# A retention and linear-attention layer on one core: the input projection by Strassen's scheme in groups of 512 columns, norm vectors on the activations, both gates at the end

## The chip, the cores and the metric

The kernel runs on one core of a Trainium2 chip. The metric is the device time of one execution in microseconds (us). The core has a matrix engine (TensorE, "PE" in the profile; its loads of the stationary operand are listed apart as "PEld"), a vector engine (VectorE, DVE), an activation engine (ScalarE, ACT), a general engine (GpSimd, POOL) and a queue that issues DMAs (SyncE, SP). Each engine takes its instructions strictly in the order in which they stand in its queue and waits on semaphores for the others. Matrix products are accumulated in PSUM (eight banks of 128 partitions x 512 float32); all else lies in SBUF.

## The reference: what is computed

One layer over 16 meta tokens and 512 tokens (T = 512, D = 1024). Cut to what matters:

```python
u = rms_norm(h, norm_gain)                 # (528, 1024)
proj = u @ w_in                            # w_in: 1024 x 11280
rq, rk, rv, rg, gq, gk, gv, gg, glr, m_ret, m_gla = split(proj)
# retention, 4 heads: q, k of 256 with rope, v and gate of 512, decay per head
o_ret = head_group_norm(retention(rope(rq), rope(rk), rv), ret_norm_gain) * silu(rg)
# gated linear attention (GLA), 4 heads: q, k of 128, v and gate of 256
log_a = log_sigmoid(glr @ w_gate_up + b_gate) / 16
o_gla = head_rms_norm(gla(gq, gk, gv, log_a), gla_norm_gain) * silu(gg)
merged = sigmoid(m_ret) * (o_ret @ w_branch_ret) + sigmoid(m_gla) * (o_gla @ w_branch_gla)
out = rms_norm(h + merged @ w_out, final_norm_gain)    # the 512 tokens
```

## The kernel before

Every large product is made of three passes in float32r: each operand is split exactly into a high and a low part (`split`, L132 to L134: a cast on ScalarE writes the high part, a subtraction on VectorE the low part), and `mm3` (L136 to L139) issues high x high, low x high and high x low into one PSUM bank. A product with 1024 rows of depth therefore takes 8 x 3 matmuls for each output tile of 128 rows.

The normalised activations stand transposed in SBUF, `uh` and `ul`: depth on partitions, 512 tokens and then 16 meta tokens in the free dimension. The weights are streamed from DRAM in tiles of 512 KB (`raw`, four buffers), each split into `_h` and `_l` tiles of 128x1024 (three buffers each). There are two forms of the projection:

- `proj_a` (L179) makes 256 columns with the columns on the partitions; the 512 tokens are the moving operand (N = 512), or 2 x 264 when the meta tokens are wanted (rk, gk). It serves rq, rk, gq, gk and the gates mr and mg.
- `proj_b` (L209) makes 512 columns with the tokens on the partitions; 512 weight columns are the moving operand (N = 512), 96 matmuls for the group. It serves rv, rg, gv, gg and the output projection wo. For rv and gv 16 small native-float32 matmuls (rv_pm, gv_pm) add the meta rows.

`branch` (L243) multiplies the gated output of an attention by its branch weights (br for a retention head, bg for a GLA pair): 96 matmuls with N = 512. Here the norm gains act on the weights: each quarter of a weight tile, 128x256, is scaled by ScalarE (L249) and by VectorE (L250) while it is split.

The order in time is written out by the generators: `weave` (L148) puts one step of a chain of small dependent work after each step of dense products. Then a scheduler orders each engine's queue from that. Stage by stage: gv0; gq0 and gk0 with the forget gates' chain (L344 to L392) woven into both; gg0 with GLA attention 0; gq1 and gk1 with the GLA output 0; gv1; gg1 and the branch bg0 with GLA attention 1; the gate mg (four `proj_a` of 256 columns) with GLA output 1; bg1, whose result is multiplied by the gate in `acc` (L584, L585); then for each head rq and rk (rope at L614; for heads 1 to 3 woven with the attention of the head before, followed by that head's branch br), rg with the scores, and rv; the gate mr with the attention of head 3; br3; wo.

The attention of a head (`ret_attention`, L698) makes four blocks of outputs (`av`, PE), their mean and variance (L715, L716), a small chain VectorE - GpSimd - VectorE, the normalised output on ScalarE (L721), the product with the gate (L722), and transposes (`ot`, L729) with a split.

PSUM is divided in two pools of four banks: `pp` for dense products, `pa` for the rest.

## Time and profile before

| | |
|---|---|
| time, median of 3 runs | 834.37 us (834.16 to 834.43) |
| span of the profiled execution | 832.0 us; its median time is 2.37 us above that |
| instructions in the trace | 10218 |
| longest stage by kind | a group of 512 columns takes 22 to 25 us of PE, and there are 21 such groups in the projection beside gv0 |
| DMA | 74.42 MB, 89 GB/s on average |

The page gives, for each engine, the time in which it was busy, its share of the span and its number of instructions. Matmuls are pipelined: the trace gives each a duration that is longer than the distance to the next one, so the pace of TensorE is read from the starts of consecutive matmuls and not from their durations. A group's row reads: line, engine, operation, output <- inputs (buffer numbers left out), shapes, count | busy us, mean ns of one | idle time of the engine just before them and what ended it. The stage table gives for a stretch of the span the busy time of each engine in it; "PEclk" is the clock granted to TensorE as a share of full speed.

### The profile page before, as it was taken

The page shows a single profiled execution, that of the slowest core. Times are in us where ns is not written, and L with a number is a line of the kernel's source. Part 1 is how long each engine was busy: PE and PEld are TensorE (multiplying, and loading weights), DVE is VectorE, ACT ScalarE, POOL GpSimd, SP SyncE. Part 2 cuts the span into 40 slices and gives each one's busy share as a digit, 9 for nine tenths or more (in the row PEclk, how much of TensorE's full clock was granted, in tenths as well). Part 3 has the DMA queues.
Part 4 walks back from the last instruction along what each step waited for, and adds up shares of the span by engine and source line. Part 5 has one row for each costly group of instructions (what it writes and reads, how often), then busy time and mean ns, then how long its engine had stood idle before and what let it go on. Part 6 is the DMA issues. An engine that isn't in the chain of part 4 may idle for free.

```text
span 832.0 us, 10218 instructions
## 1 busy us (share of the span) xinstructions
PE 814.9 (98%) x4018; PEld 665.2 (80%) x4018; DVE 420.4 (51%) x701; ACT 309.9 (37%) x563; POOL 119.6 (14%) x162
## 2 busy tenths in 40 slices
PE   7999999999999999999999999999999999999996
PEld 4779879778788889877988779888788887888885
DVE  3475564237542366415764247742467433546832
ACT  5473453245533323223432233322334233343422
POOL 5401330014300002100210002200022000221031
PEclk9999999999999999999999999999999999999999
DMA  8242110140223234214232051320512204242302
GB/s 259 67 145 78 51 52 26 60 144 27 74 79 99 81 105 146 74 39 145 60 97 68 26 176 51 102 76 26 177 51 87 92 26 145 84 176 76 126 1 101
DMA packets 57784, 74.42 MB, mean 89 GB/s; under 512 B 6708, under 2 KB 39732, under 8 KB 57736
## 3 DMA queue, kind: packets, MB, share of 16 engines
q1 hardware_dynamic: 57736, 73.78, 27.8%
q8 instruction: 31, 0.51, 0.3%
q14 instruction: 17, 0.14, 0.0%
HBM read 71.67 MB, written 2.10 MB: 89 GB/s over the span
## 4 chain that ended last, share of the span: by engine, by line
PE 92%; DVE 2%; ACT 2%; POOL 1%; issue 1%; DMA 1%; SPq 0%; POOLq 0%; DVEq 0%; ACTq 0%
PE rv_p L137 4%; PE rv_p L138 4%; PE rg_p L138 4%; PE rg_p L139 4%; PE rv_p L139 4%; PE rg_p L137 4%; PE br_p L138 4%; PE br_p L139 4%; PE br_p L137 3%; PE rk_p L137 2%; PE rk_p L138 2%; PE rk_p L139 2%; PE rq_p L137 2%; PE mr_p L137 2%; PE wo_p L138 2%; PE mg_p L139 2%
## 5 line engine op out<-in xcount | busy, mean ns | idle before, releaser
L145 POOL TENSOR_TENSOR g_r<-g_v,mhalf 128x1 f32<-128x1 f32 x16 | 8.8, 550 | 320.8 <-DVE g_v L144 320.8
L137 PE MATMUL rv_p<-rv_h,uh 128*128 128x512 f32 x128 | 50.9, 398 | 0.0
L138 PE MATMUL rv_p<-rv_l,uh 128*128 128x512 f32 x128 | 50.6, 396 | 0.0
L138 PE MATMUL rg_p<-rg_l,uh 128*128 128x512 f32 x128 | 50.6, 396 | 0.0
L139 PE MATMUL rg_p<-rg_h,ul 128*128 128x512 f32 x128 | 50.4, 394 | 0.0
L139 PE MATMUL rv_p<-rv_h,ul 128*128 128x512 f32 x128 | 50.4, 394 | 0.0
L137 PE MATMUL rg_p<-rg_h,uh 128*128 128x512 f32 x128 | 50.4, 394 | 0.0
L139 PE MATMUL br_p<-oh,br_l 128*128 128x512 f32 x128 | 50.2, 393 | 0.0
L138 PE MATMUL br_p<-ol,br_h 128*128 128x512 f32 x128 | 50.2, 392 | 0.0
L137 PE MATMUL br_p<-oh,br_h 128*128 128x512 f32 x128 | 49.8, 389 | 0.0
L134 DVE TENSOR_TENSOR rv_l<-rv_w,rv_h 128x1024 fp32r<-128x1024 f32 x16 | 19.6, 1226 | 42.7 <-ACT rv_h L133 42.2
L137 PE MATMUL rk_p<-uh,rk_h 128*128 128x264 f32 x128 | 37.1, 290 | 0.0
L138 PE MATMUL rk_p<-ul,rk_h 128*128 128x264 f32 x128 | 36.4, 284 | 0.0
L139 PE MATMUL rk_p<-uh,rk_l 128*128 128x264 f32 x128 | 36.3, 284 | 0.0
L250 DVE SCALAR_TENSOR_TENSOR br_l<-br_w,rgain,br_h 128x256 fp32r<-128x256 f32 x64 | 32.7, 555 | 5.8 <-ACT br_h L249 5.8
L133 ACT CAST rg_h<-rg_w 128x1024 fp32r<-128x1024 f32 x16 | 16.8, 1051 | 49.4 <-PE br_p L138 37.9
L249 ACT ACTIVATE br_h<-br_w,rgain 128x256 fp32r<-128x256 f32 x64 | 28.5, 501 | 11.8 <-PE mr_p L138 7.3
L721 ACT ACTIVATE on<-av,nm,g_r 128x512 f32<-128x512 f32 x16 | 12.5, 780 | 53.9 <-DVE nm L719 53.9
L137 PEld LDWEIGHTS rv_p<-rv_h,uh 128*128 128x128 f32 x128 | 24.0, 188 | 9.0 <-issue 3.4
L139 PEld LDWEIGHTS rv_p<-rv_h,ul 128*128 128x128 f32 x128 | 24.0, 187 | 5.8
L139 PEld LDWEIGHTS rg_p<-rg_h,ul 128*128 128x128 f32 x128 | 24.0, 188 | 5.6
L138 PEld LDWEIGHTS rv_p<-rv_l,uh 128*128 128x128 f32 x128 | 24.0, 188 | 5.4
(296 smaller groups left out, 2255.1 us busy)
## 6 DMA issues: line engine op xcount, KB each, us to landing
rg_w<-in_w_in_dram SPq DMA_DIRECT2D x16, 512.0 KB, 3.5
rv_w<-in_w_in_dram SPq DMA_DIRECT2D x16, 512.0 KB, 3.5
br_w<-in_w_branch_ret_dram SPq DMA_DIRECT2D x16, 512.0 KB, 3.9
gv_w<-in_w_in_dram SPq DMA_DIRECT2D x8, 512.0 KB, 7.2
gg_w<-in_w_in_dram SPq DMA_DIRECT2D x8, 512.0 KB, 3.6
bg_w<-in_w_branch_gla_dram SPq DMA_DIRECT2D x8, 512.0 KB, 3.5
mg_w<-in_w_in_dram SPq DMA_DIRECT2D x8, 512.0 KB, 3.7
rq_w<-in_w_in_dram SPq DMA_DIRECT2D x8, 512.0 KB, 4.3
```

Source lines behind the costliest of these rows:

```text
L133: nc.scalar.copy(hi, src)
L134: eng.tensor_sub(lo, src, hi.bitcast(F32))
L137: nc.tensor.matmul(o, lh, rh, start=first, stop=False)
L138: nc.tensor.matmul(o, lh, rl, start=False, stop=False)
L139: nc.tensor.matmul(o, ll, rh, start=False, stop=last)
L145: nc.gpsimd.tensor_tensor(r[:rows], v[:rows], mhalf[:rows], op=ALU.pow)
L249: nc.scalar.activation(hi[:, k, :], raw[:, k, :], AF.Copy, scale=g)
L250: nc.vector.scalar_tensor_tensor(lo[:, k, :], raw[:, k, :], g, hi[:, k, :].bitcast(F32), op0=ALU.mult, op1=ALU.subtract)
L721: nc.scalar.activation(on, ps, AF.Identity, scale=r, bias=nm)
```

## The change

**Quads.** The 21 groups of 512 columns other than gv0 (rq+rk, rg and rv of four heads; gq+gk of two pairs; gg0, gg1, gv1; mr and mg, two each) are made by a new function `quad`. The 1024-deep product of 512 tokens and 512 columns is cut in 2 x 2 blocks of 512 deep by 256, and seven products of blocks (numbered 1 to 7 in the code, issued in the order 1, 2, 7, 6, 5, 3, 4) stand for the eight. Each has 24 matmuls with N = 256, or 264 where the meta tokens are wanted ("wide"): 168 for the group. It first loads four blocks `blk[kh, n]` of 128x1024 into the ring of raw tiles. Its core:

```diff
+    def quad(cols, rows, name, evac, meta=None, wide=False):
...
+        product(1, A11, blk[0, 0], "b", True)
+        x1 = copy("b", 1)
+        run_late()
+        yield
+        t2 = wraw(f"{name}_t2")
+        product(2, A12, blk[1, 0], "a", True)
+        nc.vector.tensor_sub(blk[0, 0], blk[0, 1], blk[0, 0])
+        nc.vector.tensor_sub(blk[0, 1], blk[1, 1], blk[0, 1])
+        nc.vector.tensor_sub(t2, blk[1, 1], blk[0, 0])
+        out(0, 0, "a", x1)
+        yield
+        product(7, S3, blk[0, 1], "c", True)
+        yield
+        product(6, S2, t2, "b", False)
+        nc.vector.tensor_sub(blk[1, 0], blk[1, 0], t2)
+        x2 = copy("b", 2)
...
+        yield
+        product(5, S1, blk[0, 0], "b", False)
+        out(1, 1, "c", copy("b", 3))
+        run_late()
+        yield
+        product(3, S4, blk[1, 1], "b", False)
+        out(1, 0, "b", None)
+        yield
+        product(4, A22, blk[1, 0], "c", False)
+        out(0, 1, "c", x2)
+        yield
```

`product` splits its 128x1024 weights and accumulates 24 matmuls in a bank; products 1, 6, 5 and 3 accumulate in the same bank b, products 7 and 4 in bank c. `copy` is a ScalarE copy of bank b into SBUF between two of these products. `out` gives a quadrant of the result to the caller, with a bank and, for three of the four, a copy to be added to it on VectorE. The raw ring has six buffers instead of four; the `_h` and `_l` rings keep three.

**Activations.** In place of `uh` and `ul` there are the blocks A11, A12, A22 and A21 and the sums S1 to S4 of blocks, each split (`fh`, `fl`). The sums are formed once, behind the pre-norm: four VectorE operations and four splits.

**Norm vectors.** A function `turn` transposes the gated output of an attention by halves of the tokens and applies the gain while it splits (ScalarE 128x256 and VectorE 128x256, eight of each for a head), and `branch` now splits its weights plainly:

```diff
-            for k in range(4):
-                g = gain[:, gcol + k:gcol + k + 1]
-                nc.scalar.activation(hi[:, k, :], raw[:, k, :], AF.Copy, scale=g)
-                nc.vector.scalar_tensor_tensor(lo[:, k, :], raw[:, k, :], g, hi[:, k, :].bitcast(F32),
-                                               op0=ALU.mult, op1=ALU.subtract)
+            split(hi, lo, raw)
```

**Gates.** mg moves from the GLA part to the end, behind mr: `gates()` makes mr0, mr1, mg0, mg1 as quads, woven with the attention of head 3. The GLA branch's sum is stored to DRAM (`kept`) and loaded again at the end; GLA output 1 now runs between the attention and bg1 with nothing woven in:

```diff
-    weave(gate_gla(range(KD // 2)), gla_output(1))
-    drain(gla_branch(1))
+    drain(gla_output(1))
+    drain(gla_branch(1))
...
-    weave(gate_ret(), ret_attention(3))
+    weave(gates(), ret_attention(3))
```

**How the order of the work moves.** Queue rows: PE 3767 to 5008, DVE 624 to 878, ACT 471 to 672, POOL 133 to 146, SP 160 to 170. Three places:

VectorE in the first group with q and k of the GLA (gq0, gk0), where the forget gates' chain is woven in (la, fg_z and acc are its tiles; gq_6_l is the low part of product 6's weights). Before, only the last block of the chain stood among the gk splits:

```order
L134 TENSOR_TENSOR gvm_l<-gv_pm,gvm_h 128x512
L382 TENSOR_SCALAR la<-z_540 128x512
L385 TENSOR_SCALAR fg_z<-sigm 128x512
L134 TENSOR_TENSOR gk_0_l<-gk_0_w,gk_0_h 128x1024
L386 SCALAR_TENSOR_TENSOR fg_z<-fg_z,sigm 128x512
L134 TENSOR_TENSOR gk_1_l<-gk_1_w,gk_1_h 128x1024
L387 TENSOR_TENSOR la<-la,fg_z 128x512
L392 TENSOR_TENSOR la<-la,sigm 128x512 x5
```

In the changed kernel the rows from the last blocks of the chain to its end are:

```order
L491 TENSOR_SCALAR la<-z_622 128x512
L496 TENSOR_TENSOR la<-la,fg_z 128x512
L494 TENSOR_SCALAR fg_z<-acc 128x512
L513 TENSOR_TENSOR gq_570<-gq_a_641,gq_x_610 128x256
L495 SCALAR_TENSOR_TENSOR fg_z<-fg_z,acc 128x512
L513 TENSOR_TENSOR gq_570<-gq_a_642,gq_x_610 128x256
L496 TENSOR_TENSOR la<-la,fg_z 128x512
L141 TENSOR_TENSOR gq_6_l<-gq_t_636,gq_6_h 128x1024
L141 TENSOR_TENSOR gq_5_l<-gq_w_572,gq_5_h 128x1024
L501 TENSOR_TENSOR la<-la,acc 128x512 x5
L141 TENSOR_TENSOR gq_3_l<-gq_w_578,gq_3_h 128x1024
```

The whole chain (its first rows stand just ahead of these) now lies between the start of this group and product 6's low part, and its last five rows ahead of product 3's.

ScalarE in the gates, at the change from one group to the next. Before, a cast of weights and the sigmoid of a bank alternate with the attention's work (sigr is the gate, oh the transposed output):

```order
L133 CAST oh_5798<-ot_5986 128x4x128
L758 ACTIVATE sigr_5926<-mr_p_5933 128x512
L133 CAST oh_5798<-ot_6014 128x4x128
L133 CAST mr_0_h<-mr_0_w 128x1024
L758 ACTIVATE sigr_5926<-mr_p_5973 128x512
L133 CAST mr_1_h<-mr_1_w 128x1024
```

Now, from product 4's weights of mr1 to product 7's of mg0 (mr1_x2 and mr1_x3 are the copies of bank b behind products 6 and 5):

```order
L140 CAST mr1_4_h_7574<-mr1_w10_7378 128x1024
L228 COPY mr1_x2_7509<-mr1_b0_7388 128x512
L140 CAST mg0_1_h_7613<-mg0_w00_7605 128x1024
L228 COPY mr1_x3_7539<-mr1_b0_7388 128x512
L894 ACTIVATE sigr3_7018<-sigr3_7018 128x2x256
L140 CAST mg0_2_h_7645<-mg0_w10_7607 128x1024
```

Each copy of bank b stands behind a cast of later weights, whose buffer becomes free when the same product ends that the copy waits for.

VectorE while q and k of a head are made beside the attention of the head before (rp: rope; b, mv, nm: the norm's statistics). Before, around the last split of rope for k:

```order
L134 TENSOR_TENSOR ql1_3237<-rpq10_2_3386,qh1_3236 128x512
L250 SCALAR_TENSOR_TENSOR br0_0_l_3592<-br0_0_w_3590,rgain_84,br0_0_h_3591 128x256 x4
L715 BN_STATS b603_3451<-av03_3437 128x6
L716 BN_AGGR mv03_3452<-b603_3451 128x2
L144 TENSOR_SCALAR g03_v_3455<-mv03_3452 128x1
L719 SCALAR_TENSOR_TENSOR nm03_3459<-mv03_3452,g03_r_3456 128x1
L722 TENSOR_TENSOR on03_3461<-on03_3461,sg0_2906 128x512
```

Now, between products 5 and 4:

```order
L760 TENSOR_TENSOR rp_2_3793<-qs_3789,cs 128x256
L761 TENSOR_TENSOR rp_3_3794<-qs_3787,cs 128x256
L867 BN_STATS b_3813<-av_3805 128x6
L141 TENSOR_TENSOR rq_3_l<-rq_w_3698,rq_3_h 128x1024
L141 TENSOR_TENSOR ql_3689<-rp_0_3791,qh_3688 128x256
L141 TENSOR_TENSOR ql_3689<-rp_2_3793,qh_3688 128x256
L868 BN_AGGR mv_3814<-b_3813 128x2
L867 BN_STATS b_3867<-av_3856 128x6
```

The small rows of the statistics and of rope now stand in one queue with the 128x1024 splits of products 3 and 4.

More of the change, by code (lines that the diff above doesn't have):

```diff
@@ L407, in meta @@
             G["vm", p] = vm
-        yield from proj_b(w_in, C_GV + p * 512, uh, ul, f"gv{p}", lambda t, ps: nc.scalar.copy(v[:, t, :], ps), meta)
+        if p == 0:
+            yield from proj_b(w_in, C_GV, left, "gv0", lambda t, ps: nc.scalar.copy(v[:, t, :], ps), meta)
+        else:
+            yield from quad((C_GV + p * 512, C_GV + p * 512 + 256), True, f"gv{p}", rows_into(v), meta)
     def gla_g(p):
@@ L736, in ret_attention @@
         yield
-        turn(0)
         values(2)
         yield
-        turn(1)
+        turn(sg, 0, oh, ol, rgain, h * 4, f"ot{h}")
         yield
@@ L766, in evac @@
             if h == 0:
[L767 removed]
+                nc.scalar.copy(acc2[:, c, :], ps)
             elif h < 3:
```

392 lines of the change are left out of this document (251 added, 141 removed).

## The prediction

> **What bounds the kernel now.** First the page: its line of engines, then the chain of work that ended last.
>
> ```profile
> span 832.0 us, 10218 instructions
> PE 814.9 (98%) x4018; PEld 665.2 (80%) x4018; DVE 420.4 (51%) x701; ACT 309.9 (37%) x563; POOL 119.6 (14%) x162
> PE 92%; DVE 2%; ACT 2%; POOL 1%; issue 1%; DMA 1%; SPq 0%; POOLq 0%; DVEq 0%; ACTq 0%
> ```
>
> TensorE is busy 98% of the span and makes 92% of the chain: a matmul that goes shortens the kernel, as long as nothing else is late. VectorE has 411 us free. Then the stage table, cut where one group of products ends and the next begins; it says what each group costs and how far the other engines are from it.
>
> ```profile
> core 0: us, PE busy (x) PEld busy (x) DVE busy (x) ACT busy (x) POOL busy (x), PEclk, DMA share, GB/s
> ...
> 11.00:49.30 38.30, 35.52 (x180) 27.06 (x181) 20.67 (x32) 19.92 (x38) 16.40 (x21) 0.96 0.42 118
> 49.30:72.80 23.50, 23.50 (x148) 21.18 (x147) 17.20 (x28) 12.35 (x17) 0.00 (x0) 1.00 0.43 135
> 72.80:113.60 40.80, 39.71 (x206) 32.58 (x205) 24.20 (x47) 20.79 (x55) 15.19 (x16) 1.00 0.17 52
> 113.60:146.10 32.50, 31.35 (x194) 27.43 (x193) 16.02 (x28) 13.70 (x30) 5.56 (x8) 1.00 0.11 34
> 146.10:170.80 24.70, 24.70 (x115) 18.11 (x113) 5.33 (x5) 6.87 (x9) 0.00 (x0) 1.00 0.26 86
> 170.80:212.30 41.50, 40.26 (x210) 33.22 (x207) 25.21 (x53) 21.33 (x62) 13.92 (x16) 1.00 0.24 77
> 212.30:240.30 28.00, 27.78 (x130) 23.27 (x129) 16.82 (x33) 11.48 (x30) 5.93 (x8) 1.00 0.25 75
> 240.30:286.90 46.60, 46.60 (x210) 37.72 (x209) 14.09 (x19) 16.97 (x27) 0.00 (x0) 1.00 0.28 91
> 286.90:308.70 21.80, 21.80 (x98) 18.02 (x97) 15.11 (x24) 6.00 (x12) 0.00 (x0) 1.00 0.31 95
> 308.70:331.50 22.80, 22.80 (x146) 20.66 (x145) 14.26 (x19) 6.21 (x8) 5.30 (x5) 1.00 0.42 141
> 331.50:358.50 27.00, 27.00 (x125) 22.32 (x125) 12.85 (x20) 10.40 (x15) 3.38 (x6) 1.00 0.19 59
> 358.50:383.20 24.70, 24.70 (x114) 18.11 (x112) 7.20 (x8) 7.38 (x10) 0.00 (x0) 1.00 0.28 86
> 383.20:416.20 33.00, 33.00 (x201) 29.17 (x198) 23.07 (x49) 13.01 (x24) 6.21 (x8) 1.00 0.28 91
> 416.20:438.20 22.00, 22.00 (x98) 18.06 (x97) 13.80 (x24) 6.50 (x13) 3.01 (x6) 1.00 0.33 104
> 703.20:758.00 54.80, 54.80 (x249) 44.44 (x246) 27.86 (x48) 20.25 (x33) 11.35 (x11) 1.00 0.40 135
> ```
>
> In order: gv0, gq0+gk0, gg0, gq1+gk1, gv1, gg1, bg0, mg, bg1, rq+rk of head 0, its rg, its rv, rq+rk of head 1 with attention 0 (I call this stage A; it comes three times), a branch, mr with attention 3. From rv0 on TensorE does not pause.
>
> **What a matmul costs.** Durations overlap, so I take distances. The branch stage at 416 us holds 96 matmuls with N = 512 and nothing else to speak of: 22.00/96 = 0.229 us. For the narrow ones the timeline of rk, first and last of 36 consecutive matmuls with N = 264:
>
> ```profile
> 319.82 0.28 PE L137 MATMUL rk_p<-uh,rk_h 128*128 128x264 f32 x1
> ...
> 324.06 0.29 PE L139 MATMUL rk_p<-uh,rk_l 128*128 128x264 f32 x1
> ```
>
> (324.06 - 319.82)/35 = 0.121 us, and 256/264 of that, 0.118, is my estimate for N = 256. A group of 512 columns was 96 x 0.229 = 22.0 us and becomes 168 x 0.118 = 19.8: 2.2 gained, 15 times. A group of q and k was 48 x 0.229 + 96 x 0.121 = 22.6 and becomes 168 x 0.121 = 20.4: 2.2 gained, six times. Together 46 us. That is the most the products can give.
>
> This rests on the load of each stationary operand staying hidden:
>
> ```profile
> L137 PEld LDWEIGHTS rv_p<-rv_h,uh 128*128 128x128 f32 x128 | 24.0, 188 | 9.0 <-issue 3.4
> ```
>
> A load lasts 188 ns, more than the 121 ns between two rk matmuls, and still those go at 121: loads overlap each other or the matmuls. Were a load the pace, a group would take 168 x 0.188 = 31.6 us. The Trainium skill, page "TensorE: Matmul & The Clock Gate", section "Back-to-back issue gap", says that the spacing in a stream of loads and matmuls is set by both together, which speaks against halving N; its section "LDWEIGHTS (loading the stationary operand)" gives P/1.2, 107 ns for 128 columns, as the load. By that figure the floor would be 168 x 0.107 = 18.0 us for a group and the sum would stand; the rk rows agree so far as they go.
>
> **What the quads add elsewhere.** The rows that price it:
>
> ```profile
> L134 DVE TENSOR_TENSOR rv_l<-rv_w,rv_h 128x1024 fp32r<-128x1024 f32 x16 | 19.6, 1226 | 42.7 <-ACT rv_h L133 42.2
> L769 DVE TENSOR_TENSOR acc<-acc,br_p 128x512 f32<-128x512 f32 x16 | 11.0, 686 | 16.0 <-PE br_p L139 16.0
> L619 DVE TENSOR_TENSOR rpk<-rk_p,cs 128x264 f32<-128x264 f32 x8 | 3.4, 424 | 0.0
> L715 DVE BATCH_NORM_STATS2 b<-av 128x6 f32<-128x512 f32 x16 | 11.1, 696 | 3.5 <-PE av L712 3.4
> L250 DVE SCALAR_TENSOR_TENSOR br_l<-br_w,rgain,br_h 128x256 fp32r<-128x256 f32 x64 | 32.7, 555 | 5.8 <-ACT br_h L249 5.8
> L722 DVE TENSOR_TENSOR on<-on,sg 128x512 f32<-128x512 f32 x16 | 11.1, 691 | 11.0 <-ACT on L721 11.0
> L133 ACT CAST rg_h<-rg_w 128x1024 fp32r<-128x1024 f32 x16 | 16.8, 1051 | 49.4 <-PE br_p L138 37.9 <-PE rg_p L139 6.0 <-PE rq_p L138 4.5
> L409 ACT COPY gv<-gv_p 128x512 f32<-128x512 f32 x8 | 4.7, 589 | 4.7 <-PE gv_p L139 4.7
> L390 ACT ACTIVATE sigm<-sigm,one 128x2560 f32<-128x2560 f32 x1 | 2.4, 2441 | 0.0
> L386 DVE SCALAR_TENSOR_TENSOR fg_z<-fg_z,sigm 128x512 f32<-128x512 f32 x5 | 3.3, 683 | 0.0
> ```
>
> A group had four splits and now has seven, and four subtractions of the same 128x1024: 11 x 1.226 = 13.5 us of VectorE, and three sums of quadrants, 3 x 0.686 = 2.1. That is 15.5 against 19.8 of TensorE: covered where nothing else is in the stage. ScalarE gets 7 x 1.05 + 3 x 0.59 = 9.1. Extra in all: 21 x (15.5 - 4.9), about 220 us on VectorE; it would stand at some 640 of 820.
>
> *The copies of bank b.* Product 5 may not write bank b before the copy behind product 6 has read it, and product 3 waits likewise for the copy behind 5. No row of before has a matmul that waits for such a copy; the price lies between nothing (other matmuls stand between) and the drain of the last matmul (its 0.28 duration less the pitch: 0.16), the copy (0.59) and two hand-overs of some 0.03 (between the first two rows of the next fence): 0.8 us each. In rv the first is half covered by the two matmuls of the meta rows' sum, so 0.4 + 0.8 = 1.2 for a group; in rg, in A and in gg other matmuls cover them. In the gates the copy stands behind a cast of 1.05 on ScalarE, as the order shows, so 1.8 each, uncovered in mr1, mg0 and mg1: 6 x 1.8 = 10.8 us. I take these, near the upper end, since TensorE's queue is in order and has nothing else there.
>
> *gq0 with the forget gates.* The chain's matmuls leave gv0, which falls from 38.3 to about 33.5, and enter gq0: 20.4 + 4.8. Its VectorE rows (five blocks of four operations of up to 0.69, ready only after the bank's product and ScalarE's steps) stand ahead of product 6's low part; I walk the queue and find product 6 some 7 us late, product 3 about 1 more (the logarithm of 2.44 and five subtractions stand ahead of its split), and the copies 3.3, being all exposed there: 36.5 us. The bounds are 25 (chain hidden) and 42 (no overlap at all). While TensorE waits, its clock may fall; the row in which it idled shortly at the start:
>
> ```profile
> 13.00:17.00 4.00, 3.86 (x14) 3.44 (x15) 2.82 (x6) 2.53 (x5) 2.50 (x3) 0.57 1.05 333
> ```
>
> The granted clock was 0.57 for those 4 us. A repeat behind a 7 us wait would cost 1.7 us (4 x 0.43), which I leave to the range. The Trainium skill, the same page, section "The HAM clock gate", puts the threshold at one idle window of about 3.4 us; by that rule the 7 us wait would halve the clock and the sum would be 1.7 higher.
>
> *Stage A.* How rows follow each other on VectorE there, a dependent pair and an independent one:
>
> ```profile
> 388.62 0.70 DVE L715 BATCH_NORM_STATS2 b<-av 128x6 f32<-128x512 f32 x1 [0.59 <-PE av L712]
> 389.35 0.18 DVE L716 BATCH_NORM_AGGREGATE mv<-b 128x2 f32<-128x6 f32 x1
> ...
> 396.25 0.69 DVE L722 TENSOR_TENSOR on<-on,sg 128x512 f32<-128x512 f32 x1 [0.85 <-ACT on L721]
> 396.86 0.68 DVE L134 TENSOR_TENSOR ol<-ot,oh 128x512 fp32r<-128x512 f32 x1
> ```
>
> The first pair loses 0.03, the second overlaps by 0.08. TensorE: 33.0 - 22.6 = 10.4 of attention, and 20.4: 30.8 us. VectorE: 13.5, six half sums (2.5), rope with 16 products of 0.42 (6.8) and eight subtractions (3.7), 26.5; attention's statistics four times 0.70 + 0.69 + 0.5 of small ones, 7.6; the turn's eight of 0.555, 4.4: 38.5. Some 2.5 of it is done ahead of the stage, and of its 60 or so rows most overlap by 0.08 (about 4 in all): 32. So the two are level, and I take 32.5, between 30.8 and 36.
>
> *Norm vectors.* A branch had eight scaled quarters of each kind for two tiles and now has plain halves; TensorE sets it at 22.0 before and after, as VectorE's 13.8 there says. The turn's work is in A.
>
> *Gates.* mr with attention was 54.8 and mg 46.6, 101.4 together. The four quads take 4 x 19.8, attention 10.4 and the copies 10.8: 100.4. GLA output 1 was hidden by mg; alone it takes about 2.8 (four products of 0.69 ahead of the first transpose; the second turn lies beside bg1's splits). Storing and loading 2 MB each way, spread over 21 us and 40 us, lies beside DMA shares of 0.3.
>
> **The sum**, against the profiled 832.0: gv0 -4.8; gq0 +13.0; gg0 and gq1 -2.2 (4.4 of matmuls less half of it in waits, as VectorE goes from 24.2 to 35 of 39 and from 16.0 to 28 of 31); gv1 -1.0; gg1 and bg0 -1.0; mg to GLA output -43.8; rq0 -2.2; rg0 0.0 (the last quadrant's rope holds the scores by 2.5); rv0 -1.0; three times A -0.5, branch 0, rg -2.2, rv -1.0, that is -11.1; mr to gates +45.6; br3 and wo 0. Together -8.5: a span of 823.5. The median of the runs lies 2.4 above the span of before, so 825.9 us.
>
> **The rivals.**
> - *All hidden.* The 46 us come nearly whole: 832.0 - 46 + 2.4 = 788; with half of my stalls (gq0's 11, the gates' 10.8, A's 5, rv's and gv1's 6) still there, about 804. For it: VectorE's total stays under 80%. Against: queues in order, whose late rows the order shows. 788 to 812.
> - *VectorE's queue becomes the bound* (the other side). In A and in the two GLA attention groups small links of a chain stand behind splits of 1.226 us, and what they release on TensorE stands ahead of dense products. Price: if neighbours do not overlap and each link loses a hop, A takes 38 (+5.5, three times) and gg0 and gg1 4 more each: 823.5 + 24.5 = 848.0 span, 850 us. It decides from 8.5 us, 1.7 us in each of those five stages: then the gain is gone. For it: 38.5 us of VectorE for 30.8 of TensorE. 836 to 864.
> - *Nothing remains:* gain and waits cancel within 0.2% (about what a measurement of this kernel can tell from no change), 832.7 to 836 us.
> - *The loads set the pace:* 21 x (31.6 - 22) = +200 us, by the 188 ns row; the rk rows exclude it almost.
>
> **How the numbers follow.** Partial gain (812 to 832) 0.46; all hidden 0.16; nothing 0.06; VectorE's queue 0.31; loads 0.01. So faster 0.62, same 0.06, slower 0.32. The predicted 825.9 is that of the likeliest case. The range for eight in ten leaves out the better half of the hidden case, 0.08, and the worse part of the queue case, 0.12: 800 to 850. Since both signs hold much of the chance, the likeliest case's own range beside it is 812 to 832.
>
> **What would show it.** Distances of 0.118 between matmuls of a quad would prove the pace; a distance near 0.188 would refute everything. A line of TensorE's waits with product 6 of gq0 on its low part, of 5 us or more, and in the gates a wait of about 1.8 for the copies, twice a quad, would prove the stalls. Stage A at 32 to 33 us with VectorE busy over 30 would prove that the two are level; at 36 or more, with TensorE waiting for VectorE, the queue rival is right. If TensorE is busy all through A and the gates, the hidden case is.

## The result and the profile after

The changed kernel takes **841.49 us** (median of 4 runs, 841.39 to 842.99) where the kernel before takes 834.26 (833.97 to 834.43) on the same chip: a ratio of 1.0092, with a 95% interval of 1.008 to 1.0105. It is slower by 0.9%; the forecast said faster by 1%. The span of the profiled execution is 839.8 us, 7.8 above the 832.0 of before, where the sum gave 823.5.

The page's line of engines:

```profile
span 839.8 us, 13348 instructions
PE 784.0 (93%) x5322; PEld 703.9 (84%) x5322; DVE 619.5 (74%) x893; ACT 422.8 (50%) x707; POOL 133.7 (16%) x170
```

TensorE has lost 31 us of busy time, as it should with an eighth fewer products, and its share has gone from 98% to 93%: it now waits. VectorE stands at 619.5 us, where some 640 were forecast. The stage table, cut at the same places of the program:

```profile
core 0: us, PE busy (x) PEld busy (x) DVE busy (x) ACT busy (x) POOL busy (x), PEclk, DMA share, GB/s
11.00:43.60 32.60, 30.83 (x144) 23.06 (x144) 25.38 (x31) 22.35 (x45) 16.54 (x21) 0.90 0.51 138
43.60:82.10 38.50, 29.91 (x211) 28.10 (x208) 33.53 (x52) 23.28 (x39) 0.00 (x0) 0.91 0.24 69
82.10:181.30 99.20, 93.55 (x704) 87.17 (x702) 74.05 (x114) 61.25 (x126) 24.96 (x27) 0.98 0.22 65
181.30:219.20 37.90, 35.91 (x261) 33.02 (x260) 29.20 (x47) 26.57 (x52) 10.11 (x11) 1.00 0.28 84
219.20:275.10 55.90, 54.37 (x254) 44.47 (x253) 30.39 (x53) 22.80 (x48) 8.02 (x10) 1.00 0.28 87
275.10:298.00 22.90, 21.08 (x169) 20.55 (x168) 16.83 (x27) 10.77 (x17) 5.17 (x6) 1.00 0.49 158
298.00:351.00 53.00, 50.23 (x398) 45.66 (x399) 44.24 (x57) 27.27 (x39) 4.25 (x8) 1.00 0.30 90
351.00:384.40 33.40, 30.31 (x221) 28.57 (x220) 28.50 (x57) 17.15 (x29) 8.02 (x10) 1.00 0.31 95
384.40:407.20 22.80, 22.80 (x99) 17.98 (x98) 16.43 (x22) 9.80 (x17) 3.59 (x7) 1.00 0.16 47
...
666.00:766.30 100.30, 91.65 (x724) 87.97 (x723) 80.03 (x98) 51.56 (x69) 13.99 (x10) 1.00 0.44 137
```

In order: gv0; gq0 and gk0; gg0, gq1, gk1 and gv1; gg1; bg0, GLA output and bg1; rq and rk of head 0; its rg and rv; stage A of head 1; a branch; the four gates. Beside the forecast, as changes against before in us (a stage of before is the sum of its rows in the prediction's table; the three heads are the time from the end of rv of head 0 to the start of the gates, 320.0 before and 315.0 now):

| stage | forecast | measured |
|---|---|---|
| gv0 | -4.8 | -5.7 |
| gq0 | +13.0 | +15.0 |
| gg0 to gv1 | -3.2 | +1.2 |
| gg1 to bg1 (mg gone) | -44.8 | -44.1 |
| rq of head 0 | -2.2 | +0.1 |
| rg and rv of head 0 | -1.0 | +1.3 |
| three heads | -11.1 | -5.0 |
| gates and br3 | +45.6 | +45.6 |
| wo | 0 | -0.6 |
| sum | -8.5 | +7.8 |

The gates came out at 100.3 where 100.4 was forecast. The 16.3 us between the sums lie in four places: gg0 to gv1 (4.4), the first head's groups (2.3 and 2.3), the three heads (6.1) and gq0 (2.0). That is 17.1; the other stages take 0.8 less than forecast.

What TensorE waits for, from the trace's list of waits (total us, times, longest):

```profile
PE ot L337 <- DVE sg L874: 10.1, 7, 1.8
PE gq_b L221 <- DVE gq_l L141: 5.1, 1, 5.1
PE rv_b L221 <- ACT rv_x L228: 3.5, 8, 0.7
PE mg_b L221 <- ACT mg_x L228: 3.1, 2, 1.6
PE gc L610 <- DVE gS L664: 3.0, 2, 1.5
...
PE mg_b L221 <- ACT mg_h L140: 2.1, 2, 1.1
PE mr_b L221 <- ACT mr_x L228: 1.9, 2, 1.5
...
PE rq_b L221 <- ACT rq_x L228: 1.0, 1, 1.0
```

Rows that end in `_x L228` are waits for a copy of bank b, and the row that ends in `mg_h L140` is one for a cast of weights. `gq_b <- gq_l` is product 6 of gq0 on its low part: 5.1 us, where a walk of the queue gave 7. The transposes of an attention (`ot`) wait for the product with the gate on VectorE. The timeline of mg shows the pace and one copy:

```profile
731.25 0.28 PE L221 MATMUL mg_b<-fh,mg_l 128*128 128x256 f32 x1
733.08 0.39 PE L221 MATMUL mg_b<-fh,mg_h 128*128 128x256 f32 x1 [1.56 <-ACT mg_x L228]
733.31 0.28 PE L221 MATMUL mg_b<-fl,mg_h 128*128 128x256 f32 x1
733.43 0.28 PE L221 MATMUL mg_b<-fh,mg_l 128*128 128x256 f32 x1
...
734.48 0.28 PE L221 MATMUL mg_b<-fh,mg_l 128*128 128x256 f32 x1
```

From 733.43 to 734.48 the matmuls with N = 256 start 0.117 us apart, and 0.118 over a whole product of mg (24 matmuls from 722.85 to 725.57), as estimated: the products are as cheap as forecast. Between 731.25 and 733.08 lie 1.83 us, one pitch and 1.7 of wait; the forecast had 1.8.

### The profile page after: what moved, and what is told of

It is laid out like the page before. It is cut to its first block, busy times and chain, and to the rows that moved or that the text cites. A ratio compares the mean times of both kernels' runs of the same rounds, so it can differ in the third digit from the quotient of the medians.

```text
span 839.8 us, 13348 instructions
## 1 busy us (share of the span) xinstructions
PE 784.0 (93%) x5322; PEld 703.9 (84%) x5322; DVE 619.5 (74%) x893; ACT 422.8 (50%) x707; POOL 133.7 (16%) x170
## 5 line engine op out<-in xcount | busy, mean ns | idle before, releaser
L152 POOL TENSOR_TENSOR g_r<-g_v,mhalf 128x1 f32<-128x1 f32 x16 | 10.1, 630 | 305.7 <-DVE g_v L151 305.7
L140 ACT CAST rg_h<-rg_w 128x1024 fp32r<-128x1024 f32 x24 | 25.3, 1052 | 45.8 <-PE br_p L145 24.2
L140 ACT CAST rq_h<-rq_w 128x1024 fp32r<-128x1024 f32 x24 | 25.3, 1053 | 34.4 <-PE bg_p L145 13.0
L221 PE MATMUL rv_b<-rv_h,fh 128*128 128x256 f32 x128 | 37.0, 289 | 3.5 <-ACT rv_x L228 3.5
L221 PE MATMUL rq_b<-fh,rq_h 128*128 128x264 f32 x128 | 36.9, 288 | 1.0 <-ACT rq_x L228 1.0
L221 PE MATMUL rg_b<-rg_h,fh 128*128 128x256 f32 x128 | 36.6, 286 | 0.9 <-DVE rp L760 0.9
L221 PE MATMUL rq_b<-fh,rq_l 128*128 128x264 f32 x128 | 36.6, 286 | 0.0
L221 PE MATMUL rq_b<-fl,rq_h 128*128 128x264 f32 x128 | 36.3, 283 | 0.0
L221 PE MATMUL rv_b<-rv_l,fh 128*128 128x256 f32 x128 | 36.0, 281 | 0.0
L221 PE MATMUL rg_b<-rg_l,fh 128*128 128x256 f32 x128 | 36.0, 281 | 0.0
L221 PE MATMUL rv_b<-rv_h,fl 128*128 128x256 f32 x128 | 36.0, 281 | 0.0
L221 PE MATMUL rg_b<-rg_h,fl 128*128 128x256 f32 x128 | 35.9, 281 | 0.0
L141 DVE TENSOR_TENSOR rq_l<-rq_w,rq_h 128x1024 fp32r<-128x1024 f32 x24 | 30.4, 1266 | 3.9 <-ACT rq_h L140 3.9
L140 ACT CAST rv_h<-rv_w 128x1024 fp32r<-128x1024 f32 x24 | 24.8, 1053 | 12.2 <-DVE rv_w L252 5.6
L144 PEld LDWEIGHTS br_p<-oh,br_h 128*128 128x128 f32 x128 | 23.8, 188 | 8.2 <-ACT br_h L140 1.2
```

The costliest lines, as they stand in the source:

```text
L140: nc.scalar.copy(hi, src)
L141: eng.tensor_sub(lo, src, hi.bitcast(F32))
L144: nc.tensor.matmul(o, lh, rh, start=first, stop=False)
L152: nc.gpsimd.tensor_tensor(r[:rows], v[:rows], mhalf[:rows], op=ALU.pow)
L221: nc.tensor.matmul(ps, l, r, start=first and j == 0, stop=last and j == 2, skip_group_check=not fresh or (t == 1 and not wide))
```

## The experiments

Each ratio is against the kernel before, run on the same chip, with its 95% interval; the changed kernel's is 1.0092. Kernels are the changed one with an edit unless said otherwise. W and V in the expectations are the theory on trial (a list of separate waits) and its rival (VectorE's queue as the bound); L, in the later ones, is a theory of the attention's latency.

### Is it the copies of bank b?

**no_copies**: the copies behind products 6 and 5 are left out and the first copy is added in their place, so three of the four quadrants of each group hold other sums.

```diff
-        x2 = copy("b", 2)
+        x2 = x1
...
-        out(1, 1, "c", copy("b", 3))
+        out(1, 1, "c", x1)
```

> The changed kernel without the copies of bank b behind products 6 and 5: the first copy stands in their place, so the sums of quadrants are of other values (this part of the computation is changed, nothing else). Products 5 and 3 then wait for no copy. Theory W (the matmul gain is there and is given back in a list of separate waits, each with its own cause): the gates lose about 9 us of waits, the four rv and gv1 1.2 each, the others 2 together: 824 to 828 us. Rival V (the length of VectorE's queue is the bound, whatever ScalarE does): TensorE waits for VectorE a little later instead, 836 to 841 us.

Measured: 822.67 us, ratio 0.9868 (0.9852 to 0.9883), span 819.6: 20.2 us of span for 42 copies, 0.48 us each (18.8 us by the medians). Its stages:

```profile
81.20:174.30 93.10, 89.14 (x696) 84.22 (x695) 71.54 (x113) 56.78 (x112) 20.99 (x24) 1.00 0.22 69
...
270.20:291.20 21.00, 21.00 (x170) 20.59 (x169) 16.69 (x27) 9.57 (x13) 4.58 (x6) 1.00 0.55 177
...
342.10:377.10 35.00, 31.77 (x221) 29.97 (x220) 31.05 (x60) 16.35 (x27) 10.04 (x10) 0.95 0.29 91
...
655.30:745.50 90.20, 89.28 (x724) 87.47 (x724) 81.91 (x101) 47.62 (x61) 13.60 (x10) 1.00 0.45 146
```

The gates lose 10.1 us, which the forecast had (10.8). But gg0 to gv1 lose 6.1, rq of head 0 1.9 and its rg and rv 2.1 (50.9): places where "other matmuls cover them" had been assumed or nothing priced. In the list of waits of the changed kernel the rows of the copies (the four shown and 0.4 for `gq_b`) make only 9.9 us; a listed wait is a little short, as in mg's row, 1.56 of a gap of 1.7. Stage A does not gain: 35.0, where it was 33.4, and 35.0 again in the next head, where the granted clock does not fall.

The 6.1 us are not all the copies' own. By the starts of matmuls, gg0's products save 0.6, gq1's last three 0.7 and gv1 1.4; some 3.1 arise at one place between gg0 and product 2 of gq1. VectorE there, in the changed kernel:

```profile
119.60 1.03 DVE L141 TENSOR_TENSOR lal<-la,lah 128x256 fp32r<-128x256 f32 x1
120.55 1.21 DVE L141 TENSOR_TENSOR gq_l<-gq_w,gq_h 128x1024 fp32r<-128x1024 f32 x1
121.69 0.47 DVE L664 SCALAR_TENSOR_TENSOR gS<-gS,gto,gsu 128x256 f32<-128x256 f32 x1
122.08 1.21 DVE L141 TENSOR_TENSOR gq_l<-gq_w,gq_h 128x1024 fp32r<-128x1024 f32 x1
123.21 0.47 DVE L664 SCALAR_TENSOR_TENSOR gS<-gS,gto,gsu 128x256 f32<-128x256 f32 x1
```

and without the copies, where the scheduler has ordered the same rows otherwise:

```profile
118.71 1.08 DVE L664 SCALAR_TENSOR_TENSOR gS<-gS,gto,gsu 128x256 f32<-128x256 f32 x2
119.71 0.15 DVE L151 TENSOR_SCALAR gr_v<-gss 128x1 f32<-128x1 f32 x1
...
119.97 0.43 DVE L141 TENSOR_TENSOR lal<-la,lah 128x256 fp32r<-128x256 f32 x1
```

The update of the attention's state (`gS`) stands behind the weight splits of gq1 in the one and ahead of them in the other. In the changed kernel TensorE's next block waits 1.5 us for it (`gc <- gS`), and the clock falls behind the pause (time, busy time, clock):

```profile
120.00:124.00 4.00, 2.35 (x18) 2.01 (x17) 4.00 (x8) 1.97 (x4) 0.52 (x2) 1.00 0.00 0
124.00:128.00 4.00, 4.00 (x22) 4.00 (x22) 2.89 (x8) 3.56 (x10) 1.11 (x3) 0.57 0.45 133
```

That is 1.7 us of clock and 1.5 of wait. It is the mechanism that the prediction's slower rival names, a link of a chain behind a split, at one place. The same thing goes the other way in gg1: without the copies it takes 40.4 us for 37.9, with a wait of 1.9 for `lal` and a clock of 0.57 from 184 to 188 us. So a copy costs (20.2 - 3.1)/42 = 0.41 us if only the gain is taken out, and 0.47 if the loss in gg1 is added back; both are estimates.

**copies_first** keeps the copies but moves each ahead of the cast that stood before it on ScalarE (the casts of product 4 and of the next group's product 1 are issued behind the copy).

```diff
+        with tc.issue_after(c2):
+            product(4, A22, blk[1, 0], "c", False)
```

> The changed kernel, with the same work, but ScalarE's queue puts the copy of bank b ahead of the cast of later weights wherever the cast stood ahead of it (product 4's cast behind the copy of product 6, the next group's first cast behind the copy of product 5). Theory W: six copies in the gates come 1.05 us earlier, and the waits there fall from about 1.6 to 0.7: 835 to 837 us. Rival V: no effect beyond 1 us, 840.5 to 842.

Measured: 835.3 us, 1.0019 (1.0009 to 1.003), 6.2 below the change, as W had it. mg's waits for a copy fall to 0.7 at most. So about a third of what no_copies gains is the copies' place behind a cast.

**order_1267543** puts another bank's product between a product in b and the next one there: product 7 behind 6 and product 4 ahead of 3, with the third copy taken from bank c. The subtraction that makes product 6's weights (`t2`) moves up with it.

```diff
+        nc.vector.tensor_sub(t2, blk[1, 1], blk[0, 0])
         nc.vector.tensor_sub(blk[0, 1], blk[1, 1], blk[0, 1])
-        nc.vector.tensor_sub(t2, blk[1, 1], blk[0, 0])
...
-        product(7, S3, blk[0, 1], "c", True)
         yield
         product(6, S2, t2, "b", False)
...
         x2 = copy("b", 2)
+        yield
+        product(7, S3, blk[0, 1], "c", True)
+        x3 = copy("c", 3)
...
         product(5, S1, blk[0, 0], "b", False)
-        out(1, 1, "c", copy("b", 3))
+        out(1, 1, "b", x3)
...
+        product(4, A22, blk[1, 0], "c", False)
+        out(0, 1, "c", x2)
         yield
         product(3, S4, blk[1, 1], "b", False)
         out(1, 0, "b", None)
-        yield
-        product(4, A22, blk[1, 0], "c", False)
-        out(0, 1, "c", x2)
```

> The changed kernel with the seven products in another order, 1, 2, 6, 7, 5, 4, 3, so that between any two products of bank b stands one of another bank, and the third copy is of bank c behind product 7; same number of instructions, same result. Theory W, in the form that the run without copies gave it (a copy costs the wait and the emptying of the matmul pipeline, some 19 us in all): nearly all of that is hidden, 822 to 826 us. Rival: the copies and sums only move to where the next thing waits for them (weights of product 6 are needed one product earlier), 835 us or more.

Measured: 829.42 us, 0.9945 (0.9928 to 0.9963): 12.1 us below the change, and short of what W wanted by 3.4. Its heads and gates:

```profile
344.40:378.40 34.00, 30.26 (x220) 28.51 (x219) 30.33 (x59) 16.48 (x28) 8.95 (x9) 1.00 0.29 93
378.40:403.30 24.90, 23.41 (x100) 17.97 (x99) 16.69 (x22) 10.40 (x18) 5.05 (x8) 1.00 0.14 43
...
661.50:754.00 92.50, 89.60 (x724) 87.58 (x724) 82.42 (x101) 51.58 (x69) 14.55 (x10) 1.00 0.45 146
```

The gates take back 7.8 of their 10, with all copies still made. Stage A and its branch go the other way: 58.9 together, where the change has 56.2.

### Is it the amount of work on VectorE?

**no_weight_sums** leaves out the four subtractions of weight blocks (product 6 takes `blk[1, 1]`), so the products are others; 84 instructions of 128x1024 go.

```diff
-        nc.vector.tensor_sub(blk[0, 0], blk[0, 1], blk[0, 0])
-        nc.vector.tensor_sub(blk[0, 1], blk[1, 1], blk[0, 1])
-        nc.vector.tensor_sub(t2, blk[1, 1], blk[0, 0])
...
-        nc.vector.tensor_sub(blk[1, 0], blk[1, 0], t2)
```

> The changed kernel without the four subtractions of weight tiles in each quad: products 7, 6, 5 and 4 are fed with plain blocks (this part of the computation is left out). VectorE has 21 x 4.9 = 103 us less, nothing else moves. Rival V: every stage in which VectorE was near the bound shrinks, head stages with q and k from 33.4 to 31, the GLA groups by 2 to 3 each, the group of gq0 by 8: 815 to 823 us. Theory W: only the waits that VectorE ends shrink, the 5.1 of gq0 (and the clock that falls behind it) and part of the 10 of the transposes: 829 to 835 us.

Measured: 841.06 us, 1.0083 (1.0067 to 1.01). The page:

```profile
span 837.4 us, 13251 instructions
PE 781.5 (93%) x5322; PEld 704.0 (84%) x5322; DVE 528.8 (63%) x809; ACT 420.2 (50%) x707; POOL 123.7 (15%) x170
```

VectorE is 90.7 us less busy, and the time is 0.4 us less. Both expectations fell: with its rows in this order, how much VectorE has to do does not set the time. The waits of product 6 in gq0 (5.1) and of `gc` for `gS` (2.8 in all for 3.0) are still there.

### The forget gates

**no_forget_math** leaves out the arithmetic of the chain behind its matmul (ScalarE's absolute value, exponential and logarithm, and all VectorE rows but the clip); the log gates are then only the clipped linear values.

> The changed kernel without the elementwise steps of the forget gates behind their matmuls, except one per block (this part of the computation is left out). It prices the chain in gq0: theory L and W both expect the group of gq0 to fall from 38.5 us to 26 to 30 with the half clock gone, 829 to 833 us in all. If it stays above 838, the 15 us by which that group grew have another cause.

Measured: 830.29 us, 0.9957 (0.9942 to 0.9971), 11.2 below the change. gv0 and gq0:

```profile
11.00:43.70 32.70, 30.77 (x144) 23.17 (x144) 25.38 (x31) 22.46 (x45) 16.60 (x21) 0.90 0.50 138
43.70:73.30 29.60, 27.35 (x211) 26.10 (x208) 22.98 (x32) 14.71 (x27) 0.00 (x0) 1.00 0.30 90
```

gq0 falls from 38.5 to 29.6, and its mean granted clock rises from 0.91 to 1.00. In the changed kernel the windows around product 6's wait read:

```profile
64.00:68.00 4.00, 0.00 (x0) 0.00 (x0) 4.00 (x9) 1.45 (x3) 0.00 (x0) 0.77 0.00 0
68.00:72.00 4.00, 3.27 (x15) 3.27 (x16) 3.37 (x5) 2.64 (x2) 0.00 (x0) 0.50 0.51 144
```

TensorE does nothing for 4 us while VectorE is busy throughout, and then runs at half clock for 4 us: about 2 us lost, which the forecast had left to the range. The Trainium skill, page "TensorE: Matmul & The Clock Gate", section "The HAM clock gate", says that one idle window of about 3.4 us halves the clock; these rows agree.

**forget_later** lets the chain begin four steps of the weave later.

```diff
-    weave(run(gla_v(0), gla_qk(0)), forget_gates(), 4)
+    weave(run(gla_v(0), gla_qk(0)), forget_gates(), 8)
```

> The changed kernel, with the forget gates' chain woven four steps later, so that on VectorE the low parts of products 7, 6, 5 and 3 of gq0 stand ahead of the chain's bulk instead of behind it. Theory W: product 6's wait of 5.1 us, two smaller ones and the half clock behind them go, 7 to 10 us: 831 to 835 us. Rival: the chain's end is what matters, and the GLA attention behind it waits as long as product 6 did: 838 to 842 us.

Measured: 838.13 us, 1.0048 (1.0032 to 1.0063): 3.4 less, as the rival had it. The wait in gq0 is gone, and the attention behind it, which needs the gates, takes longer in turn.

**forget_own_memory** answers another thought: the chain's loads are issued at 39.2 us where before they went at 27.3, because SP waits 6.2 us at this line, until VectorE is done with the older tiles on the same bytes (`s`, L442; GpSimd's memset of `fg_f` waits 5.3 us for the same row):

```profile
L460 SPq DMA_DIRECT2D fg_f<-in_w_in_dram x1: 368/368/368, 39.2 to 39.2; - x1
```

The chain's inputs get memory of their own.

```diff
+    fg = [ap.tile([P, 641], F32, name="fg_f"), ap.tile([P, KD, P], F32R, name="fg_w")]
...
-        f = gp.tile([P, NTB, 512], F32, tag="goh", name="fg_f")
+        f, wls = fg
```

> The changed kernel, with the weights of the forget gates (641 and 1024 columns) in memory of their own instead of on the bytes of the tiles in which the activations' sums are formed. In the changed kernel these loads were issued at 39.2 us, behind the last sum, and before at 27.3. Theory W, corrected after the run with the later chain (which gained 3.4 us of the 7 to 10 expected: the end of the chain is needed by the GLA attention): it is the late start that costs; the chain's matmuls return to gv0, the wait of 5.1 us and the half clock behind it go, 830 to 834 us. Rival V: VectorE is full between 40 and 70 us anyway, so that the chain delays splits of gv0's end and gq0 as much: 838 to 842 us.

Measured: 842.43 us, 1.0094 (1.0079 to 1.0109). No gain: the late loads are real, but not what costs. VectorE is then busy almost without a pause from 36 to 56 us, and gv0 with gq0 takes 73.6 where it took 71.1.

### Parts alone

**before_norm_on_outputs** is the kernel before with only the norm vectors moved (`turn` and the plain split in `branch`); **norm_on_weights** is the changed kernel with that part undone.

```diff
-                nc.scalar.activation(hi[:, k, :], raw[:, k, :], AF.Copy, scale=g)
...
+            split(hi, lo, raw)
```

> The kernel before with one part of the change alone: the norm vectors act on the attention's output (turns by halves of the tokens, gain in the split), and the branch weights are split plainly. Theory W: the transposes wait for two blocks at once, so the waits of the changed kernel (10 us) appear in good part here too, and the branch keeps its 22 us: 837 to 843 us. Rival: this part is free, since VectorE is far from full here and the waits of the changed kernel come with the quads: 833 to 835 us.

> The changed kernel with one part undone: the norm vectors act on the branch weights again, and the outputs are turned block by block, as before. The part alone cost 4.9 us on the kernel before. Theory W (latency: a turn by halves waits for two blocks): the transposes' waits of 10 us fall to under 3, 833 to 836 us. Rival V (with the quads VectorE is full, and the scaled splits bring some 16 us back to it): 839 to 843 us.

Measured: 838.85 us, 1.0059 (1.0037 to 1.0081), so the part costs the kernel before some 5 us; and 847.14, 1.0151 (1.0136 to 1.0166), so undoing it costs the changed kernel another 5.6. The second is above both expectations. Both can hold: alone, the turn makes A longer (34.1 for 33.0); undone in the changed kernel, A takes 34.4 and the branch 24.4 (23.6 in the next head, where the clock does not fall), and its list of waits has a new row:

```profile
PE br_p L144 <- ACT oh L140: 8.1, 3, 2.7
```

**before_gates_last** is the kernel before with only mg moved to the end (its own `proj_a`).

```diff
-    weave(gate_gla(range(KD // 2)), gla_output(1))
+    drain(gla_output(1))
```

> The kernel before with one part of the change alone: the gate mg is made at the end, behind mr, in its old form of four projections, and the GLA output 1 runs with nothing woven in (the GLA sum stays in SBUF). Theory W: the GLA output costs what it now exposes, four products, transposes and splits, 3 to 6 us, and the gates cost the same wherever they stand: 837 to 840 us. Rival: the place of the gate is free, as the first branch after it covers the output: 834 to 835.

Measured: 834.97 us, 1.0012 (1.0003 to 1.0022), 1.0 more than the kernel before on that chip, as the rival had it. bg0 to bg1 take 3.3 more (the GLA output stands bare), and the gates with br3 give 1.8 back.

### Stage A and its branch

Stage A and its branch take 55.0 before and 56.2 in the changed kernel, for a forecast of 54.5. Four runs ask which dependence it is.

**turn_later** puts the fourth block's values ahead of the first turn.

```diff
+        values(3)
+        yield
         turn(sg, 0, oh, ol, rgain, h * 4, f"ot{h}")
         yield
-        values(3)
```

> The changed kernel, with the first turn of a head's output woven one step later (behind the fourth block of outputs) and the second turn one step later too. The profile of the changed kernel has 10.1 us of TensorE waits of the transposes for the product with the gate. Theory W: these are latency of a chain that is asked for too early, and 6 to 9 us of them go: 832 to 836 us. Rival: the chain is late because VectorE's queue is full, and what is asked for later is late again (the branch then waits): 839 to 842 us.

Measured: 852.99 us, 1.0226 (1.0208 to 1.0245); its stages were not recorded in a comparable execution. Both expectations missed by far. The granted clock of its executions of 852 to 853 us was 0.978, where the change has 0.988 to 0.992. Some 0.012 of 851 us is 10 us, so the clock may hold most of the 11.5 us by which it is above the change; no trace shows it.

**attention_cut_off** writes the product with the gate to a tile of its own, so that the transposes read the plain gate and depend no more on the statistics (the head's output lacks the attention).

```diff
-            nc.vector.tensor_mul(sg[:, ib, :], on, sg[:, ib, :])
+            nc.vector.tensor_mul(on, on, sg[:, ib, :])
```

> The changed kernel, with the retention's transposes fed with the gate alone instead of with the product of gate and normalised output (this part of the computation is changed; every instruction is still there, in the same queues, but the transposes and the branch do not depend on the attention's chain any more). Theory L (the latency of the chain from one block of outputs to the transposes bounds the stage with q and k): its 10 us of waits, with the emptied pipeline some 12, go, and a head's q and k take 31 instead of 33.4: 828 to 833 us. Rival V (VectorE's queue bounds it): the splits and turns stand in the same queue, the waits move to the branch or to rope, 837 to 842 us.

Measured: 843.13 us, 1.011 (1.0089 to 1.0131), a little above both expectations. A is 32.4, the branch 23.8: 56.2 again. The wait has only moved on, to the branch's banks:

```profile
PE br_p L144 <- DVE rp L760: 6.6, 3, 2.2
```

**branch_behind_gate** (with the new order and the late turn) weaves rq, rk and rg together with attention and scores, and puts the branch behind rg; **branch_behind_gate_forget_later** adds the weave of 8.

```diff
-            weave(ret_qk(h), ret_attention(h - 1), skip=0)
+            weave(run(ret_qk(h), ret_g(h)), run(ret_attention(h - 1), pause(1), ret_scores(h)))
```

> All work kept, same result. The kernel with the product order 1, 2, 6, 7, 5, 4, 3 (829.4 us), and for heads 1 to 3 the attention of the head before and then the scores are woven into q, k and gate products together, the branch follows behind the gate; turns one step later. Theory L: the attention's latency has 14 products to lie beside instead of 7, and the branch finds its input ready: a head takes 99 to 101 us instead of 105.7, so 812 to 818 us. Rival V: the same work stands on VectorE in the same 105 us, less than 2 us gained: 827 to 830 us.

> The kernel before this one in the list, with the forget gates' chain woven four steps later too (that alone gained 3.4 us on the changed kernel). If the costs are separate, 2 to 4 us less than that kernel; if the end of the chain is now what the GLA attention waits for, no difference.

Measured: 840.8 us, 1.008 (1.006 to 1.01), 11 above the new order alone, against both expectations; and 837.07, 1.0041 (1.0026 to 1.0056). In the first the scores now wait for k:

```profile
PE sc L144 <- ACT kh L140: 14.6, 4, 4.2
```

Behind such waits the clock falls: it was 0.60 and 0.55 in the two windows of 4 us from 380 to 388 us, around the end of one of 4.2 us. TensorE's busy time times the missing share of the clock, added up over windows of 4 us, gives an estimate of 16 us lost to the clock in this run and of 6 in the new order alone. By that estimate most of the 11 us lie there.

Over the runs, the first A and branch together: no copies 57.4, no weight sums 57.9, norm on weights 58.8, new order 58.9, attention cut off 56.2. In the first three the clock fell at one place of these stages (0.74, 0.62 and 0.62 in a window of 4 us); the next heads of the same runs, where it did not, take 57.4, 56.9 and 58.0. Whatever single cause goes, the two stages do not get shorter.

### Together

**three_mended** joins the new order, the norm on the weights and the forget gates' own memory; **three_mended_scores_later** starts the scores one step later.

> The changed kernel with three things mended at once: product order 1, 2, 6, 7, 5, 4, 3, the forget gates' weights in memory of their own, the norm vectors on the weights. If the three costs are separate (theory W), the gains add up: 12 from the order, 8 to 11, 5 to 8, so 810 to 817 us, below both kernels. If they share one bound (rival V), the sum falls short by more than half: over 823 us.

> The kernel with three things mended, and the scores of a head woven one step later into its gate's products. In the run with the new product order the scores waited 4.8 us for the last quadrant of k. Theory W: these waits go, 2 to 5 us below the kernel with three things mended. Rival: the scores' chain then ends later than the products that cover it, no difference within 1 us.

Measured: 840.22 us, 1.0066 (1.0049 to 1.0083), and 837.57, 1.0041 (1.0025 to 1.0057). Measured singly on the changed kernel the three parts are worth -12.1, +5.6 and +0.9 us, which would give 836.0: the first is 4.2 above that, so the parts do not add. In its list the branch waits 11.2 us in three places for the turned output (`br_p <- oh`, longest 3.7), the clock is 0.50 from 388 to 392 us behind the first, and the estimate of the loss to the clock is 17 us, 11 more than in the new order alone.

**order_where_no_rope** uses the new order only in the 15 groups without q and k; **order_where_no_rope_forget_later** adds the weave of 8.

```diff
+        if wide:
+            product(7, S3, blk[0, 1], "c", True)
+            yield
+            product(6, S2, t2, "b", False)
...
+            return
```

> All work kept, same result. The product order 1, 2, 6, 7, 5, 4, 3 only in the 15 groups without q and k; the six groups with q and k keep the order of the changed kernel. With the new order everywhere, q, k and the branch behind them took 58.9 us of a head, with the old one 56.2. If that is the order's doing (the last quadrant of k, its rope and its bank come last), the 8 us of three heads come back, less some 3 us in the first head and gq: 821 to 826 us. If it is only noise of the queues' order, 828 to 831 us, like the new order everywhere.

> The kernel before this one in the list, and the forget gates' chain woven four steps later, which gained 3.4 and 3.7 us in two other pairs. If separate: 3 to 4 us less again, 818 to 823 us.

Measured: 827.87 us, 0.9936 (0.9924 to 0.9949), and **825.42 us, 0.9904 (0.9888 to 0.9919)**: the fastest kernel that leaves nothing out, 8.5 us below the kernel before on that chip and 16.1 below the change. From the change it differs in the order of the seven products in 15 groups, with the third copy and one subtraction that follow it, and in one number. The first comes out just below its rival's 828 and the second gains 2.5 where 3 to 4 were expected: with the old order for q and k, A and the branch still take 58.0 (57.3 in the next head), so the new order there explains at most 1.6 of the 2.7 us by which it lengthened them.

## Why the prediction was wrong

- **The gain of the products** was right: 0.118 us a matmul, and TensorE is 31 us less busy. The loads of 188 ns stay hidden.
- **The gates** were right in size and cause, with one difference: each of the three uncovered groups waits 1.7 for the copy behind product 6, but only 1.2 at the copy behind product 5. There the next group's product 1 stands ahead of product 3 and waits for its cast (`mg_b <- mg_h` in the list), and the copy runs meanwhile. 10.1 us come back when two copies of each group go.
- **gv0, gv1 and the stages from gg1 to bg1** came out within 1 us: gv1 runs from 157.5 to 181.3, 23.8 for 24.7 before, as forecast (-1.0).
- **gq0** was right in its cause and 2.0 short: the wait was 5.1 for a forecast 7, and the half clock behind it, named and left out of the sum, cost 2. The copies, priced at 3.3 there, give back only 0.7 in no_copies; other waits (1.3, 1.1, 0.7 and 0.5), of which 1 was priced, make up for it, and some 2 us have no row. So this term is a sum of misses both ways.
- **The step that failed first** is "gg0 and gq1 -2.2 (4.4 of matmuls less half of it in waits, as VectorE goes from 24.2 to 35 of 39 ...)". They take 75.4 us (82.1 to 157.5) for 73.3 before: +2.1, so 4.3 off, and some 3.1 of them are the state's update behind the splits and the clock behind that wait; the copies, priced at nothing here, make up the rest (0.6 and 0.7). VectorE's share of the stage says nothing on this; the order of its rows does.
- **The step on the copies** reads "in rg, in A and in gg other matmuls cover them". In gg0 they nearly do (0.6 for both). In rq of head 0 nothing was priced at all: its products 6, 5 and 3 take 1.2 us longer than without copies, and the stage 1.9, as rg's first product also waits 0.9 for the rope, and 0.2 without copies. rg and rv of head 0 are 2.3 off and get 2.1 back. That is 4.6 us more, 4.0 of them back in no_copies.
- **Stage A** was put at 32.5, again by level totals, and the branch at its 22.0 of before. They took 33.4 and 22.8, so 1.7 a head and 5.1 for three. With 2.0, 4.3 and 4.6 this makes 16.0 of the 16.3.
- **The rival on VectorE's queue** (836 to 864) holds the result. Its mechanism, a small link behind a split, is shown between gg0 and gq1 and at product 6 of gq0; but A lost 0.9 where it asked for 5.5, gg1 nothing where it asked for 4, and as an amount of work it is refuted: 90.7 us less changed nothing. So it named the kind of loss and not where most of it is.
- **Norm vectors** were priced at nothing in the branch and 4.4 us of VectorE in A: alone, on the kernel before, they cost 4.9 us. GLA output 1 was priced at 2.8 us and costs 3.3 alone.

**What stays open:** which dependence holds A and its branch. VectorE is busy 28.5 of 33.4 us there, and its queue holds the attention's chain, the rope, the splits and the release of the branch's banks. The runs exclude its volume (in no_weight_sums it is busy 38.1 us in the two stages for 44.9, without gain), the copies and the transposes' dependence on the statistics as the single cause, and the cut-off shows one wait come back at the next. Whether the order of VectorE's rows there is the cause, as between gg0 and gq1, was not tried row by row.

## What to carry to other kernels

When a sum of products is kept in one bank and read between them, put another bank's product behind each read: the same work went from 841.5 to 829.4 us by this order. Where a small chain shares an in-order engine with long rows, read which long row stands ahead of each link and what TensorE has queued behind it; the engine's share of busy time told nothing here. A wait of TensorE can cost twice, once itself and once in the clock behind it, so read the granted clock of each stage beside the list of waits. Costs found by single removals do not add in stages tied by such chains, and a removal can change the scheduler's order elsewhere: compare the order before the gain is put down to what was removed.

## What the runs showed of the hardware

The granted clock fell to 0.57 for 4 us (124 to 128, shown above) when TensorE had idled only 1.65 of the 4 us before, at most 1.51 at a stretch; in that stretch it also ran small matmuls in float32. The Trainium skill, page "TensorE: Matmul & The Clock Gate", section "HAM oscillation — how this bites in real kernels", asks for no idle gap above some 3.4 us; none was here, and the clock fell all the same. A wait as long does not always do it: the other wait of 1.5 us for `gS`, in gg1, and one of 1.4 for `lal`, between 88 and 92 us, were followed by a clock of 1.00. What decides stays open.

And the branch after stage A, at full clock and without a wait of TensorE in the list, takes 22.8 us (99 matmuls) where it took 22.0 (98) before. About half of that is the pace: its matmuls with N = 512 start 0.233 us apart, and 0.229 before. They also start 0.233 apart in no_copies and 0.229 apart in before_norm_on_outputs, so neither the copies nor the norm vectors make the difference; no run told what does.
